# Moving two parts of a modulation product from the end of a recurrent loop to the stage ahead of the attention

## The chip, the cores and the metric

The kernel runs on one core of one Trainium2 chip. The metric is the device time of one execution in microseconds. A core has TensorE (PE), VectorE (DVE), ScalarE (ACT), GpSimd (POOL) and SyncE (SP); each takes its instructions in the order of its own queue. SP here issues nearly all plain transfers, GpSimd the gathers by index; 16 DMA engines carry them.

## The reference

A block of two layers over 512 latent tokens and a prefix of 256 context tokens, width 1024, all in float32. Each layer has six modulation vectors for the latents and six for the context, products of a condition vector with a weight of 1024 x 6144:

```python
for layer in range(DEPTH):                     # 2 layers
    m_l = split((silu(c) @ mod_w[layer] + mod_b[layer]), 6)
    m_c = split( silu(c_ctx) @ mod_w[layer] + mod_b[layer], 6)
    a_l = modulate(rmsnorm(h_lat, norm1_g[layer]), m_l[0], m_l[1])
    a_c = modulate(rmsnorm(h_ctx, norm1_g[layer]), m_c[0], m_c[1])
    # layer 0: RWKV-7 heads and S5 groups; layer 1: latent attention
    o_c, o_l = mixer(a_c, a_l)
    h_lat = h_lat + m_l[2] * o_l
    f_l = modulate(rmsnorm(h_lat, norm2_g[layer]), m_l[3], m_l[4])
    h_lat = h_lat + m_l[5] * moe_ffn(f_l)      # layer 0: context likewise
return rmsnorm(h_lat, final_g)
```

The six vectors of a layer come in three parts of two (2048 columns each): part 0 holds vectors 0 and 1, part 1 holds 2 and 3, part 2 holds 4 and 5.

## The kernel before

The kernel is written in a tile framework. The program gives the order of work; a planner then orders each engine's queue by priority (program order, unless a block raises or lowers it) and by its own estimate of when operands are ready, and puts in the waits. A block under a run-time condition closes the queues: what stands behind it isn't moved ahead of it.

The stages in order of time: `front` (layer 0's modulation, norms, input projection), `rwkv` (six steps of two half steps, with the S5 work and the preparation of later steps in between), `concat`, `ffn(0, ...)` (output projection, router, 20 expert blocks, then `overflow`, a loop under the run-time condition `tc.If(n > 0)`), the stage that prepares the attention, `attention`, `ffn(1, ...)` and the last norm.

`mod_part(l, q, ...)` computes part q of layer l. It clears a bias tile `mb` (GpSimd, one buffer), loads the bias into it, and for 8 slices of the contraction and 2 halves loads a weight tile `mw` of 128 x 4 x 256 (512 KB, pieces of 1 KB) through SP and multiplies it (line 164): four matmuls with a stationary operand of 128 x 32, one for each quarter of TensorE's columns, into one PSUM bank `psmod`. Then `mb` is added, the norm's weight multiplied in, and the rows stored to DRAM (`mods`). In the loop, layer 1's three parts are placed by

```python
MODN = {3: (0,), 4: (1,), 5: (2,)}
```

behind steps 3, 4 and 5, with three buffers for `mw`. Part 0 is read when the attention is prepared, parts 1 and 2 from the output projection of layer 1 on.

A step of the loop needs the inverse of small triangular matrices, made one step ahead in `rwkv_stage_b`: `X` by VectorE row after row (lines 596 and 598), stored by SP (line 601), read back as diagonal blocks `D` (line 604, 16 transfers), then a chain between TensorE and ScalarE: `Ta` (613), `W` (617), `G` (624), `Tb` (634 and 639), `G` (645). `rwkv_steps` uses it: `VU` (699), then the state `Z` (704 and 706), which the next half step begins by decaying (677).

The stage that prepares the attention begins behind `overflow`. It splits the weights (`mla_split`, lines 1600 to 1604), spreads the gate rows (`row_psum`, 1438), and for six token tiles t (two of context, four latent): `fetch` gathers two expert rows per token (GpSimd, line 1415, tiles `cy`, two buffers each), `combine` adds them to `h` (1528 to 1530), SP stores `h` for latents (2014), then the norm (`rstd_of`), its transpose (`norm_tile`, `ntt`), the down projection (`mla_down`) and the value products (`mla_values`). PSUM has eight banks: `tp`, `mm`, `ca` and `cb` with two buffers each.

Of the kernel before, what the change touches and what calls it, by code (L numbers as in the profile page):

```python
# [16 lines left out]
F32 = mybir.dt.float32  # L17
# [27 lines left out]
MS14 = (4, 0, 5, 1, 6, 2, 7, 3, 12, 8, 9, 10, 11, 13)  # L45
MODT = "lo"
S5LATE = -800
MODN = {3: (0,), 4: (1,), 5: (2,)}


def dap(ap, offset, dims):
# [36 lines left out]
class Block:  # L88
# [35 lines left out]
    def cond(self, tp):  # L124
        nc, i = self.nc, self.i
        cr = tp.tile([16, 128], F32, name="cr")
        nc.sync.dma_start(cr[0:8, :], i["c"].rearrange("b (k p) -> (b k) p", p=128))
        nc.sync.dma_start(cr[8:16, :], i["c_ctx"].rearrange("(k p) -> k p", p=128))
        cs = tp.tile([16, 128], F32, name="csil")
        nc.scalar.activation(cs, cr, AF.Tanh, scale=0.5)  # L130
        nc.vector.tensor_scalar(cs, cs, 0.5, 0.5, op0=OP.mult, op1=OP.add)
        nc.vector.tensor_tensor(cs, cs, cr, OP.mult)
        pt = self.psum("tp", "pt_c", 2)
        nc.tensor.transpose(pt[:, :16], cs, self.ident[:16, :16])
        self.cst = self.c0.tile([128, 8, 32], F32, name="cst")
        nc.gpsimd.memset(self.cst, 0.0)
        nc.vector.tensor_copy(self.cst[:, :, 0:2], pt[:, :16].rearrange("p (v k) -> p k v", v=2))

    def mod_part(self, l, q, wpool, spool, tag="mod"):

        nc, i = self.nc, self.i
        if l not in self.mods:
# [13 lines left out]
            nc.vector.tensor_scalar(mb[r0:r0 + 64, :], mb[r0:r0 + 64, :], 1.0, None, op0=OP.add)  # L156
        ps = self.psum(tag, f"psmod{l}{q}", 1)
        for k in range(8):
            for h in range(2):
                wt = wpool.tile([128, 4, 256], F32, name=f"mw{l}{q}{k}{h}", tag="mw")  # L160
                w = i["mod_w"][l, k * 128:(k + 1) * 128, q * 2048:q * 2048 + 2048].rearrange("p (j c) -> p j c", j=4)
                last = nc.sync.dma_start(wt, w[:, :, 256 * h:256 * h + 256])
                for j in range(4):
                    nc.tensor.matmul(ps[32 * j:32 * j + 32, 256 * h:256 * h + 256], self.cst[:, k, :], wt[:, j],  # L164
                                     start=(k == 0 and h == 0), stop=(k == 7), skip_group_check=True)
        mo = mb
        nc.vector.tensor_tensor(mo, ps, mb, OP.add)
# [1263 lines left out]
        nc.vector.tensor_tensor(hh, hh, ps[:, 256:], OP.mult)  # L1431
        return hh

    def row_psum(self, rows, name):

        out = [self.psum("cb", f"{name}{hf}", 2) for hf in range(2)]
        for j in range(8):
            self.nc.tensor.matmul(out[j // 4][:, j % 4 * 128:j % 4 * 128 + 128], self.ident[0:8, j:j + 1].to_broadcast([8, 128]),
                                  rows, start=True, stop=True, skip_group_check=True)
        return out  # L1440
# [174 lines left out]
    def mla_values(self, t):  # L1615

        nc = self.nc
        ts = slice(t * 128, t * 128 + 128)
        for hh in range(2):
            hs = slice(hh * 8, hh * 8 + 8)  # L1620
            ps = self.psum("ca", f"pv{t}{hh}", 2)
            self.mm3(ps, (self.kvT[0][:, ts], self.kvT[1][:, ts]), [x[:, hs, :].rearrange("p h c -> p (h c)") for x in self.kw],
                     True, True)
            dst, src = self.vv[:, t, hs], ps.rearrange("p (h c) -> p h c", h=8)
# [5 lines left out]
    def mla_down(self, aT, t, sp):  # L1630
# [8 lines left out]
        else:  # L1639
            nc.tensor.matmul(ps[:, 0:416], self.tri[0:1, 1], self.mwb, start=True, stop=False)  # L1640
            for k in range(8):
                self.mm3(ps[:, 0:416], (aT[0][:, k], aT[1][:, k]), (self.mwi[0][:, k], self.mwi[1][:, k]), False, k == 7)
        pt = self.psum("cb", f"pmt{t}", 2)
        if t >= 2:
            r = self.rstd_of(sp, ps[:, 0:256], f"mq{t}", 256)
            qn = sp.tile([128, 256], F32, name=f"qn{t}", tag="qn", bufs=2)
            nc.vector.scalar_tensor_tensor(qn, ps[:, 0:256], r, self.qnb, op0=OP.mult, op1=OP.mult)
            for k in range(2):
                nc.tensor.transpose(pt[:, k * 128:(k + 1) * 128], qn[:, k::2], self.ident)
        r = self.rstd_of(sp, ps[:, 256:384], f"mk{t}", 128)  # L1650
        kn = sp.tile([128, 128], F32, name=f"kn{t}", tag="kn", bufs=2)
        nc.vector.scalar_tensor_tensor(kn, ps[:, 256:384], r, self.kvb, op0=OP.mult, op1=OP.mult)
        nc.tensor.transpose(pt[:, 256:384], kn, self.ident)
        pe = sp.tile([128, 32], F32, name=f"kpe{t}", tag="kpe", bufs=2)
# [305 lines left out]
    def build(self):  # L1960
# [7 lines left out]
        with ExitStack() as es:  # L1968
# [10 lines left out]
            with ExitStack() as ec:  # L1979
# [5 lines left out]
        mes = ExitStack()  # L1985
        self.ffn(0, cat, hts, self.src_rows, i["hy_w_out"], ces,
                 lambda: self.mla_weights(self.pool("mlaw", 1, es=mes, side="right")))
        with ExitStack() as e0:
            kp = self.pool("mlk", 1, es=e0)
            self.rq = kp.tile([128, 2, 16, 96], F32, name="mqu")  # L1990
# [7 lines left out]
            with ExitStack() as e1:  # L1998
# [3 lines left out]
                sp = self.pool("mls", 1, es=e1, side="right")  # L2002
                g2c = [bp.tile([128, D], F32, name=f"g2c{v}") for v in range(2)]
                for v in (1, 0):
                    for hf, ps in enumerate(self.row_psum(self.g2r[:, v], f"g2c{v}")):
                        nc.scalar.activation(g2c[v][:, hf * 512:hf * 512 + 512], ps, AF.Copy)
                self.mla_split(wp)

                def normed(t):
                    h = hts[t]  # L2010
                    self.combine(self.fetch(0, t, xp, 2), h, g2c[int(t < 2)],
                                 (nc.vector, nc.vector if t < 2 else nc.gpsimd))
                    if t >= 2:
                        nc.sync.dma_start(self.hb[(t - 2) * 128:(t - 1) * 128], h)
                    r = self.rstd_of(xp, h, f"n1{t}")
                    return self.norm_tile(h, r, t, self.mc1, xp)

                nxt = normed(0)
# [148 lines left out]
```

## Time and profile before

| what | us |
|---|---|
| median of 3 runs (1953.17 to 1964.0) | 1959.4 |
| the profiled execution | 1948.41 |
| its span, first to last instruction | 1946.6 |
| TensorE busy in it | 1563.9 (80%) |
| VectorE busy in it | 1218.9 (63%) |
| granted TensorE clock, mean | 0.88 |

The profile is one execution. Its page gives the busy share of each engine, also in 40 slices of 48.7 us, and the DMA queues. The trace behind it gives windows (busy time of each engine in a stretch, the granted clock as a share of 2.4 GHz, the share of time in which the 16 DMA engines were busy and GB/s), waits (who stood idle for whom), and instructions in order of time. Times of a row count from the span's start.

### The profile page before, as it was taken

Reading aid. Unit: us, or ns where it says so; the run is one execution under the profiler, and the core shown is the slowest. Engines: PE = TensorE matmul, PEld = TensorE weight load, DVE = VectorE, ACT = ScalarE, POOL = GpSimd, SP = SyncE. Lnnn points to the kernel's source line nnn. Section 1 sums busy time; section 2 is a strip of 40 time slices with the busy share of each in tenths; the row PEclk is TensorE's granted clock in tenths of the full one; section 3 lists DMA queues with packets and bytes.
Section 4 is the critical chain, followed back from the end, with each engine's and each line's share of the span. In section 5 each row is a group of like instructions: output and inputs, shape, how many; then the busy total and the mean of one; then the engine's idle time right before and its main releaser. Section 6 shows DMA issues by size and latency. Waiting matters only on the chain. (4 is left out here: it accounts for less than half of the span.)

```text
span 1946.6 us, 32507 instructions
## 1 busy us (share of the span) xinstructions
PE 1563.9 (80%) x12531; PEld 1126.9 (58%) x12531; DVE 1218.9 (63%) x2385; ACT 774.2 (40%) x1434; POOL 701.3 (36%) x700
## 2 busy tenths in 40 slices
PE   5698898558687789649698999949699998789993
PEld 2376767447576655337575666638455556666662
DVE  4799933884866867243754654475678854575544
ACT  4222324334543523132413555433556543335542
POOL 0476802441423414102514233451143353324432
PEclk8688999678898869679899999969799998899997
DMA  8754587723233268743605999852000009349965
GB/s 257 213 174 157 164 275 218 218 60 109 62 88 103 72 223 258 241 170 128 246 33 188 389 354 367 328 175 65 1 1 1 1 0 367 110 168 370 377 230 184
DMA packets 222854, 347.65 MB, mean 179 GB/s; under 512 B 49538, under 2 KB 170296, under 8 KB 207784
## 3 DMA queue, kind: packets, MB, share of 16 engines
q1 hardware_dynamic: 206784, 294.71, 45.4%
q0 software_dynamic: 10080, 44.04, 6.3%
q10 hardware_dynamic: 5832, 6.78, 1.1%
q8 instruction: 100, 1.64, 0.3%
q14 instruction: 58, 0.48, 0.1%
HBM read 279.02 MB, written 66.46 MB: 177 GB/s over the span
## 5 line engine op out<-in xcount | busy, mean ns | idle before, releaser
L164 PE MATMUL psmod<-mw,cst 128*32 128x256 f32 x768 | 83.8, 491 | 43.5 <-DMA mw<-in_mod_w_dram 39.2
L191 PE MATMUL pwi<-aT,wih 128*128 128x256 f32 (+1 forms) x224 | 81.7, 367 | 14.4 <-DVE q L334 7.2
L192 PE MATMUL pwi<-aT,wih 128*128 128x256 f32 (+1 forms) x224 | 81.9, 367 | 0.0
L193 PE MATMUL pwi<-aT,wil 128*128 128x512 f32 (+1 forms) x224 | 81.2, 364 | 0.0
L1784 ACT ACTIVATE P<-st 128x512 f32<-128x512 f32 x96 | 56.9, 596 | 48.7 <-PE st L1782 44.7
L1797 POOL TENSOR_TENSOR sum<-sum,P 128x512 f32<-128x512 f32 x48 | 63.6, 1348 | 27.8 <-ACT P L1784 27.6
L1112 PE MATMUL s5y<-s5tq,s5H 128*96 128x128 f32 x256 | 50.6, 333 | 27.3 <-POOL s5H L1104 15.1
L1415 POOL DMA_INDIRECT xg<-fbuf,rk x36 | 37.8, 1051 | 92.9 <-PE ptx L231 52.3
L572 PE MATMUL pg<-PQ,KB 64*128 64x128 f32 x384 | 54.1, 318 | 18.7 <-ACT ta L501 10.4
L1098 POOL TENSOR_TENSOR s5t<-s5G,s5tq 128x384 f32<-128x384 f32 x16 | 18.0, 1123 | 141.5 <-DVE s5G L1095 121.3
L185 ACT ACTIVATE xT<-ptx 128x512 fp32r<-128x512 f32 x72 | 41.2, 596 | 66.1 <-PE ptx L231 65.0
L164 PEld LDWEIGHTS psmod<-mw,cst 128*32 128x32 f32 x768 | 20.3, 124 | 77.4 <-DMA mw<-in_mod_w_dram 55.7
L186 DVE TENSOR_TENSOR xT<-ptx,xT 128x512 fp32r<-128x512 f32 x72 | 48.2, 688 | 23.1 <-ACT xT L185 22.2
L572 PEld LDWEIGHTS pg<-PQ,KB 64*128 64x128 f32 x384 | 44.1, 211 | 31.2 <-ACT ta L501 10.7
L191 PEld LDWEIGHTS pwi<-aT,wih 128*128 128x128 f32 x224 | 46.2, 208 | 22.3 <-issue 11.4
L1112 PEld LDWEIGHTS s5y<-s5tq,s5H 128*96 128x96 f32 x256 | 37.8, 198 | 35.9 <-POOL s5H L1104 16.8
L1795 POOL TENSOR_TENSOR sum<-P,P 128x512 f32<-128x512 f32 x16 | 20.5, 1300 | 105.3 <-ACT P L1784 105.2
L231 PEld LDWEIGHTS ptx<-ident,xg 128*128 128x128 f32 x288 | 40.6, 192 | 26.6 <-issue 21.0
L1788 PE MATMUL po<-P,vv 128*64 128x512 f32 x192 | 54.3, 617 | 1.1 <-ACT P L1784 1.1
L685 PE MATMUL pU<-Z,PQ 128*64 128x128 f32 x192 | 30.3, 331 | 27.9 <-ACT Z L677 27.7
L231 PE MATMUL ptx<-ident,xg 128*128 128x128 f32 x288 | 42.9, 285 | 10.9 <-issue 7.0
L192 PEld LDWEIGHTS pwi<-aT,wih 128*128 128x128 f32 x224 | 46.1, 206 | 7.8 <-issue 3.1
(1569 smaller groups left out, 5161.0 us busy)
## 6 DMA issues: line engine op xcount, KB each, us to landing
mw<-in_mod_w_dram SPq DMA_DIRECT2D x96, 512.0 KB
yb<-yo SPq DMA_DIRECT2D x36, 512.0 KB
s5tq<-s5t SPq DMA_DIRECT2D x16, 960.0 KB
yb<-zrow SPq DMA_DIRECT2D x16, 512.0 KB
wi<-in_hy_w_in_dram SPq DMA_DIRECT2D x14, 512.0 KB
rk<-qbuf SPq DMA_DIRECT2D x12, 512.0 KB
fbuf<-f SPq DMA_DIRECT2D x10, 512.0 KB
s5t<-s5CP SPq DMA_DIRECT2D x4, 1152.0 KB
```

What stands on the lines that cost most here:

```text
L164: nc.tensor.matmul(ps[32 * j:32 * j + 32, 256 * h:256 * h + 256], self.cst[:, k, :], wt[:, j], start=(k == 0 and h == 0), stop=(k == 7), s ...
L185: nc.scalar.activation(hi, src, AF.Copy)
L186: nc.vector.tensor_tensor(lo, src, hi.bitcast(F32), OP.subtract)
L191: nc.tensor.matmul(out, lh, rh, start=start, stop=False, **kw)
L192: nc.tensor.matmul(out, lh, rl, start=False, stop=False, **kw)
L193: nc.tensor.matmul(out, ll, rh, start=False, stop=stop, **kw)
L231: nc.tensor.transpose(pt[:, k * 128:(k + 1) * 128], a[:, h * 4 + k::8], self.ident)
L572: nc.tensor.matmul(pg[hp][:, m], KB[rs, m, ps2], PQ[rs, m, ps2], start=True, stop=True, skip_group_check=True)
L1112: nc.tensor.matmul(out, H[:, g, d, k, h0:h0 + 96], CP[:, k, d, i0:i0 + 8, :].rearrange("p a b -> p (a b)"), start=False, stop=(d == 1 and ...
L1784: ex = nc.scalar.activation(P, st, AF.Exp, scale=SCALE)
L1788: mm = nc.tensor.matmul(po[64 * x:64 * x + 64], vv[:, kt, h0 + x, :], P, start=(kt == 0), stop=(kt == 5), skip_group_check=True)
L1797: nc.gpsimd.tensor_tensor(sums[x], sums[x], P, OP.add)
```

## The change

Only part 0 stays in the loop. Parts 1 and 2 are computed behind `ffn(0, ...)`, after the weights are split and ahead of the first token tile, with weight tiles of 128 x 4 x 128 (256 KB, pieces of 512 bytes), four a slice, and four buffers. The padded condition vector `cst` lives in a pool that closes before the experts, so its two columns are kept in `cst2` and spread again. A PSUM pool of its own serves the stage: the part's accumulator takes one bank (`md`), `cb` has three buffers and takes the value products in as well, and `ca` is gone. For room in SBUF the squares of three norms are written over tiles that are there already: a gathered tile, `qn` and `kn`.

```diff
-MODN = {3: (0,), 4: (1,), 5: (2,)}
+MODN = {3: (0,)}
...
-        nc.vector.tensor_copy(self.cst[:, :, 0:2], pt[:, :16].rearrange("p (v k) -> p k v", v=2))
-
-    def mod_part(self, l, q, wpool, spool, tag="mod"):
+        self.cs2 = self.cp.tile([128, 8, 2], F32, name="cst2")
+        nc.vector.tensor_copy(self.cs2, pt[:, :16].rearrange("p (v k) -> p k v", v=2))
+        nc.vector.tensor_copy(self.cst[:, :, 0:2], self.cs2)
+
+    def mod_part(self, l, q, wpool, spool, tag="mod", parts=2, bufs=None):
...
-            for h in range(2):
-                wt = wpool.tile([128, 4, 256], F32, name=f"mw{l}{q}{k}{h}", tag="mw")
+            for h in range(parts):
+                n = 512 // parts
+                wt = wpool.tile([128, 4, n], F32, name=f"mw{l}{q}{k}{h}", tag="mw", bufs=bufs)
...
-            ps = self.psum("ca", f"pv{t}{hh}", 2)
+            ps = self.psum("cb", f"pv{t}{hh}", 3)
...
-        pt = self.psum("cb", f"pmt{t}", 2)
+        pt = self.psum("cb", f"pmt{t}", 3)
...
+        mp = self.pool("mwp2", 1, es=mes, side="right")
+        self.cst = mp.tile([128, 8, 32], F32, name="cst1")
+        nc.gpsimd.memset(self.cst, 0.0)
+        nc.vector.tensor_copy(self.cst[:, :, 0:2], self.cs2)
+        self.ppes.close()
+        self.psum_pool(None, "ppm")
...
                 self.mla_split(wp)
+                for q in (1, 2):
+                    self.mod_part(1, q, mp, mp, "md", 4, 4)
...
-                    r = self.rstd_of(xp, h, f"n1{t}")
+                    r = self.rstd_of(xp, h, f"n1{t}", sq=ys[1])
```

## Rows read from the trace of the kernel before

**Rows 1.** The page: DMA engines' busy tenths in 40 slices of the span.

```profile
DMA  8754587723233268743605999852000009349965
```

**Rows 2.** Windows of the loop's end: length, busy us and instructions of each engine.

```profile
757.00:781.00 24.00, 19.32 (x183) 9.30 (x182) 23.52 (x75) 6.40 (x16) 10.56 (x17) 0.91 0.76 242
781.00:802.00 21.00, 14.56 (x203) 8.82 (x203) 7.28 (x15) 2.50 (x3) 5.14 (x5) 0.58 0.63 189
802.00:844.00 42.00, 28.65 (x677) 17.11 (x676) 7.13 (x15) 7.72 (x16) 0.00 (x0) 0.73 0.74 237
844.00:878.00 34.00, 11.38 (x176) 9.06 (x176) 19.09 (x39) 15.79 (x31) 0.81 (x6) 0.72 0.44 157
```

**Rows 3.** Windows, instructions on the modulation's accumulator alone: PE, PEld, DVE busy.

```profile
757.00:802.00 45.00, 15.49 (x129) 3.50 (x128) 0.68 (x1) 0.76 0.70 217
802.00:844.00 42.00, 12.17 (x120) 3.17 (x120) 0.69 (x1) 0.73 0.74 237
sum 87.00, PE 27.67 PEld 6.67 DVE 1.37; mean PE 13.83 PEld 3.33 DVE 0.68
```

**Rows 4.** Waits from 802 to 844: us in total, times, the longest.

```profile
ACT Tb L634 <- PE pt L632: 14.7, 1, 14.7
...
PE psmod L164 <- DMA mw<-in_mod_w_dram: 11.6, 7, 6.1
```

**Rows 5.** Timeline of SP's queue, 690 to 880: start, duration, instruction.

```profile
785.98 4.62 SPq L162 DMA_DIRECT2D mw<-in_mod_w_dram  x2
790.69 7.85 SPq L604 DMA_DIRECT2D D<-xo  x16
```

**Rows 6.** Timeline of ScalarE: an earlier step (two rows), then the last.

```profile
476.81 0.59 ACT L613 ACTIVATE Ta<-pd 128x512 f32<-128x512 f32 x1
...
502.84 1.21 ACT L699 ACTIVATE VU<-pU 64x512 f32<-64x512 f32 x2
...
802.08 0.60 ACT L613 ACTIVATE Ta<-pd 128x512 f32<-128x512 f32 x1 [9.55 <-PE pd L612]
...
837.81 1.21 ACT L699 ACTIVATE VU<-pU 64x512 f32<-64x512 f32 x2 [6.94 <-PE pU L697]
...
844.53 2.44 ACT L677 ACTIVATE Z<-Z,dc 128x128 f32<-128x128 f32 x8
```

**Rows 7.** Windows of the stage that prepares the attention, as in rows 2.

```profile
1276.00:1301.00 25.00, 0.31 (x3) 0.12 (x2) 18.38 (x45) 6.71 (x14) 15.15 (x9) 0.55 0.60 194
1301.00:1330.00 29.00, 24.83 (x115) 23.33 (x116) 23.73 (x57) 7.65 (x22) 17.69 (x12) 0.80 0.58 192
1330.00:1372.00 42.00, 38.39 (x177) 32.96 (x175) 22.09 (x94) 13.52 (x45) 0.20 (x1) 0.96 0.00 1
1269.00:1372.00 103.00, 70.53 (x322) 59.26 (x320) 70.65 (x228) 34.42 (x92) 35.47 (x23) 0.82 0.34 110
```

**Rows 8.** Timeline of PE at the head of that stage.

```profile
1268.59 5.75 PE L1603 MATMUL pmwb<-mwr,mcol 128*1 128x416 f32 x16 [0.30 <-PEq L1504]
...
1301.15 1.06 PE L301 MATMUL ntt<-ntd,h 128*128 128x128 f32 x3 [24.84 <-issue]
```

**Rows 9.** DMA, 328 to 342 (512-byte writes), and SP's issues, 14 to 45.

```profile
DMA packets 7921, 4.00 MB, mean 286 GB/s; under 512 B 112, under 2 KB 7921, under 8 KB 7921
...
14.43 30.50 SPq L162 DMA_DIRECT2D mw<-in_mod_w_dram  x13
```

**Rows 10.** The gathered expert rows, 1255 to 1310: durations min/median/max in ns.

```profile
L1530 POOL TENSOR_TENSOR h<-h,cy x2: 2375/2504/2633, 1297.0 to 1302.9; 128x1024 f32<-128x1024 f32 x2
...
DMA to landing us min/median/max: 4.2/5.4/6.6
```

**Rows 11.** Waits from 757 to 845, as in rows 4.

```profile
PE psmod L164 <- DMA mw<-in_mod_w_dram: 18.6, 13, 6.1
...
POOL mb L146 <- DMA mods<-mb: 10.3, 1, 10.3
```

More of the change, by code (lines that the diff above doesn't have):

```diff
@@ L158, in mod_part @@
         for k in range(8):
-            for h in range(2):
-                wt = wpool.tile([128, 4, 256], F32, name=f"mw{l}{q}{k}{h}", tag="mw")
+            for h in range(parts):
+                n = 512 // parts
+                wt = wpool.tile([128, 4, n], F32, name=f"mw{l}{q}{k}{h}", tag="mw", bufs=bufs)
                 w = i["mod_w"][l, k * 128:(k + 1) * 128, q * 2048:q * 2048 + 2048].rearrange("p (j c) -> p j c", j=4)
-                last = nc.sync.dma_start(wt, w[:, :, 256 * h:256 * h + 256])
+                last = nc.sync.dma_start(wt, w[:, :, n * h:n * h + n])
                 for j in range(4):
-                    nc.tensor.matmul(ps[32 * j:32 * j + 32, 256 * h:256 * h + 256], self.cst[:, k, :], wt[:, j],
+                    nc.tensor.matmul(ps[32 * j:32 * j + 32, n * h:n * h + n], self.cst[:, k, :], wt[:, j],
                                      start=(k == 0 and h == 0), stop=(k == 7), skip_group_check=True)
@@ L1432, in expert_mm, with row_psum @@
         return hh
-    def row_psum(self, rows, name):
-        out = [self.psum("cb", f"{name}{hf}", 2) for hf in range(2)]
+    def row_psum(self, rows, name, tag="cb", bufs=2):
+        out = [self.psum(tag, f"{name}{hf}", bufs) for hf in range(2)]
         for j in range(8):
@@ L1642, in mla_down @@
                 self.mm3(ps[:, 0:416], (aT[0][:, k], aT[1][:, k]), (self.mwi[0][:, k], self.mwi[1][:, k]), False, k == 7)
-        pt = self.psum("cb", f"pmt{t}", 2)
+        pt = self.psum("cb", f"pmt{t}", 3)
         if t >= 2:
-            r = self.rstd_of(sp, ps[:, 0:256], f"mq{t}", 256)
             qn = sp.tile([128, 256], F32, name=f"qn{t}", tag="qn", bufs=2)
+            r = self.rstd_of(sp, ps[:, 0:256], f"mq{t}", 256, sq=qn)
             nc.vector.scalar_tensor_tensor(qn, ps[:, 0:256], r, self.qnb, op0=OP.mult, op1=OP.mult)
@@ L1649, in mla_down @@
                 nc.tensor.transpose(pt[:, k * 128:(k + 1) * 128], qn[:, k::2], self.ident)
-        r = self.rstd_of(sp, ps[:, 256:384], f"mk{t}", 128)
         kn = sp.tile([128, 128], F32, name=f"kn{t}", tag="kn", bufs=2)
+        r = self.rstd_of(sp, ps[:, 256:384], f"mk{t}", 128, sq=kn)
         nc.vector.scalar_tensor_tensor(kn, ps[:, 256:384], r, self.kvb, op0=OP.mult, op1=OP.mult)
@@ L2004, in build @@
                 for v in (1, 0):
-                    for hf, ps in enumerate(self.row_psum(self.g2r[:, v], f"g2c{v}")):
+                    for hf, ps in enumerate(self.row_psum(self.g2r[:, v], f"g2c{v}", "cb", 3)):
                         nc.scalar.activation(g2c[v][:, hf * 512:hf * 512 + 512], ps, AF.Copy)
                 self.mla_split(wp)
+                for q in (1, 2):
+                    self.mod_part(1, q, mp, mp, "md", 4, 4)
                 def normed(t):
                     h = hts[t]
-                    self.combine(self.fetch(0, t, xp, 2), h, g2c[int(t < 2)],
+                    ys = self.fetch(0, t, xp, 2)
+                    self.combine(ys, h, g2c[int(t < 2)],
                                  (nc.vector, nc.vector if t < 2 else nc.gpsimd))
```

## Prediction

> **What bounds the kernel now.** The view to begin with is the page's row of DMA busy tenths [rows 1]: counted from 0, slices 14 to 17 (681 to 876 us, the end of the RWKV loop) stand at 6, 8, 7 and 4, slices 28 to 32 (1363 to 1606 us, the attention) at 0. The bytes that the change moves, 32 tiles of 512 KB or 16.8 MB, are loaded now in the first stretch, and the change puts them just ahead of the second.
>
> Next, the loop's end by windows [rows 2]. From 757 to 781 VectorE is busy 23.5 of 24 us (the triangular inverse for the last step, with the rest of the step before): that stretch is VectorE's. From 781 to 844 VectorE is nearly free (14.4 of 63 us) and ScalarE too, while TensorE is busy 43 of 63. So a chain sets the time there, and TensorE's order in it. The same windows for the modulation matmuls alone [rows 3] give 27.7 us of TensorE from 757 to 844, 12.2 of them behind 802; and the waits from 802 to 844 show TensorE standing 11.6 us more before such a matmul for its tile to land [rows 4]. TensorE takes its instructions in order, so the inverse's small matmuls stand behind both: ScalarE waits 14.7 us for one of them [rows 4].
>
> **What is removed.** The chain of the last step: X is written out, read back as the diagonal blocks (16 loads of D), then Ta, W, G, Tb, Tb, G, VU and Z. Two parts of it pay for the modulation.
> First, SP: it stands 4.6 us at two weight tiles before it can issue the D loads [rows 5]. The stall goes: 790.7 - 786.0 = 4.7 us.
> Second, from Ta (802.1) to the next decay of Z (844.5), 42.4 us [rows 6]. Modulation is in it with 12.2 us of matmuls and 11.6 us of waits, 23.8 together: the most that can come back. The least comes from an earlier step, where the way from Ta to VU took 26.0 us with other work in between, against 35.7 here: 9.7 us. Some of the 23.8 lies beside ScalarE's and VectorE's pieces of the chain; TensorE has little else here, so I take a value near the upper end, 19 us.
> Sum: 4.7 + 19 = about 24 us earlier, bounds 14 and 28.5. Behind it the stretch 844 to 878 keeps its length: its chain is Z, the outputs, their norm and the concatenation, without a modulation tile. Everything behind shifts, the experts too. The 15.5 us of modulation matmuls between 757 and 802 [rows 3] I price at nothing: up to 781 they lie beside VectorE at 98% [rows 2], and to 798 beside the D loads [rows 5]. If that cover were gone, each would cost what it takes.
>
> **What is added.** The same 16.8 MB as 64 tiles of 256 KB, on SP, behind the branch that closes the experts, and their matmuls on TensorE in the stretch 1269 to 1372 that prepares the attention. It is not idle [rows 7]: TensorE is busy 70.5 of 103 us there, and the DMA engines 0.34 of the time, 35 us. TensorE's gaps are one of 25 us (1276 to 1301, the wait for the first expert rows; [rows 7, 8]), then 4.2 and 3.6 us.
> DMA first. The nearest row for 512-byte pieces is a run of writes at 286 GB/s [rows 9]: 16.8 MB take 59 us, and with the 35 there already 94 of 103. The nearest row for this very load is the first part of layer 0: 13 tiles of 512 KB in 30.5 us, 2.35 us each, three in flight [rows 9]; by bytes that is 75 us for 64 halves, and 110 with the other traffic. With the first tiles out at about 1269, the stream ends between 1363 and 1379. I take 1368.
> TensorE next, which ends later. The matmuls have half the columns and twice the number, so their time stays 27.7 us [rows 3]. 70.5 + 27.7 = 98.2. In the gap of 25 us the gathers hold 0.60 of the DMA engines [rows 7]; the rest brings 0.40 x 25 x 286 = 2.9 MB, a sixth of the stream, 4.7 us of matmuls: 20.3 us stay empty. Of the later 7.8 us half is filled: 4 stay. 1269 + 98.2 + 24.3 = 1391.5, which is 19.5 later than 1372. On top come waits for tiles that arrive later than the order of TensorE's queue assumed: in the loop's end they were 18.6 us for the same bytes [rows 11], here most of them fall into the gap that is counted already; I take 5. Sum: 24.5 us later. It agrees with the stream: two of the four latent tiles left at 1368, at 42 / 4 = 10.5 us each [rows 7], end at 1389.
> Bounds: from below, all of the 27.7 us falls into the 32.5 us of gaps and the stream ends at 1363 with one tile to come: 2 us. From above, a stream of 113 us (first rival) with three tiles to come: 1269 + 2 for the first landing + 113 + 31.5 = 1415.5, 43 us.
>
> **The smaller edits.** The copy of the condition vector and the memset of its padded form are one small instruction each, beside the branch's first matmul of 5.8 us [rows 8]; without that cover they cost under 1 us. The PSUM banks: value products and the transposed latents now share three buffers instead of two and two. From below nothing; from above as much again as TensorE waits in 1330 to 1372 today, 3.6 us [rows 7]. The modulation's stream covers it; I take nothing. The squares are now written over a gathered tile, so its buffer comes free one addition (2.5 us on GpSimd) and one square later, for a gather that takes 5.4 us to land [rows 10]: at most four times 2.5 us, under the same cover; nothing again, and it is inside the upper bound.
> Nothing behind the attention moves: the parts are read only in the output projection after it, and the DMA engines are idle during the attention [rows 1].
>
> **Sum.** 24 us earlier, 24.5 later: no change. The profiled execution, 1948.4 us, would stay at 1949; it lies 11 us below the median of the runs, 1959.4, and carried to the median the forecast is 1960. Under 0.5%, some 10 us, a measurement of this kernel can hardly be told from no change.
>
> **The rivals.**
> 1. Slower: the stream goes by the count of tiles, not by bytes. Three in flight at 2.35 us each mean that one buffer's round (issue, landing, matmul, release) took 7.05 us [rows 9]. If the round does not shrink with the tile, four in flight give 1.76 us each, 113 us for 64, and the stage ends 43 us later: 43 - 24 = 19, 1978 us. It decides from a round of about 6.5 us on. For it: buffers that come free in the order of a busy TensorE, and the gathers on the same engines. Against it: 512-byte pieces at 286 GB/s. The Trainium skill speaks for it too (DMA: Bandwidth & Descriptors, Rules for kernel authors): for full bandwidth it asks for at least 1 MiB per DMA, and these shrink from a half to a quarter of that. The formula on the same page (Anatomy of one DMA), 2.0 us plus bytes over 436 GB/s, gives as an estimate 64 x 2.6 / 4 = 42 us against 32 x 3.2 / 3 = 34, so 8 us more and 1968; by the 512-byte row alone halving costs nothing. No row here shows a 256-KB tile of this kind.
> 2. Slower: GpSimd. The second of the two parts clears the same bias tile that the first still has to store; that memset waited 10.3 us in the loop's end [rows 11], where GpSimd had nothing to do. Now the expert rows' gathers and the additions on GpSimd stand behind it. If it lies ahead of the last of them, the price is that wait: 10 us, 1970.
> 3. Faster: the matmuls fit the gaps. If the gathers yield more of the DMA engines, most of the 27.7 us goes into the 25 us, and the stage ends some 5 us later: 5 - 24 = -19, 1940. For it: the 25 us are wholly empty, and DMA has 68 us to spare. Against it: the spare DMA time lies mostly behind 1330, TensorE's mostly before 1301.
>
> **Chances.** Forecast 0.40, by itself 1950 to 1969; first rival 0.20, second 0.13, third 0.27. Faster 0.28, no change 0.39, slower 0.33. The range holds the faster rival (1940) and the first one (1978) with some room on each side for the gain's own bounds, 14 and 28.5: 1936 to 1985. Outside lie only the cases where gain and loss are both at opposite ends (1933 and 1988).
>
> **What would show it.** In the profile after: D loads issued right behind X without a tile's stall, and Ta to the decay of Z some 23 us instead of 42; 844 to 878 unchanged in length. Then, from the end of the branch to the attention's first projections, 127 us instead of 103, with modulation matmuls of about 28 us in TensorE's busy time and some 20 us of the first gap still empty. The stream's length decides between forecast and first rival, a wait of the bias tile's memset before a gather shows the second, a full first gap the third. The prediction is wrong if the chain of the last step is held by something that hides now behind the tiles (then the gain falls toward 14), or if TensorE waits for tiles far more than 5 us outside the first gap.

## The result, and the profile after

| | before | after |
|---|---|---|
| median of 10 runs each, us | 1954.3 (1948.7 to 1964.0) | 1972.3 (1964.2 to 1977.4) |
| ratio, with its 95% interval | | 1.008 (1.0057 to 1.0102) |
| the profiled execution, us | 1948.41 | 1972.32 |

The change makes the kernel slower, by 0.8%. A second measurement of both (the last experiment) gave 1.0061 (1.0039 to 1.0084). Both intervals exclude no change; their lower ends are at 0.4 and 0.6%. Lines of the changed kernel stand 3 to 12 higher than in the kernel before (modulation matmul 167, its load 165, Ta 616, VU 702, Z 680).

**How to compare the two traces.** The order of instructions is the same in both (but for small instructions at the very start, and neighbours in TensorE's queue that change places) up to 741.8 us of the kernel before, where its loads of part 1 begin. Yet the second VU of step 3 stands at 652.1 in the one and at 660.6 in the other, and the second VU of step 4 at 748.8 and 760.0, 11.2 us apart. Over thirteen profiles of this study the latter lies anywhere from 747.7 to 765.7 (run 2, whose profiled execution was its longest, has 773.7). So the ends of two profiles say little here, and lengths between fixed instructions say more. Three stretches carry the change: *loop's end*, from the second VU of step 4 to the second VU of step 5; *experts*, from there to TensorE's first instruction behind the branch; *stage*, from there to the first projection of the attention.

| us | before | after |
|---|---|---|
| loop's end | 101.6 | 83.0 |
| experts | 418.2 | 424.0 |
| stage | 109.1 | 132.4 |
| first projection to the first gather of layer 1 | 349.6 | 351.7 |

The prediction ended the stage at the copies of the attention's first weights; by that mark it is 103.4 and 131.9 us, so 28.5 more instead of 23.3. In before these copies ran 5.7 us ahead of the first projection, which is the row that counts:

```profile
1377.66 0.76 PE L191 MATMUL pqp<-qT,qwp 128*128 128x512 f32 x1 [0.83 <-ACT ngm L1687]
```

**The loop's end after**, by windows, cut at the steps of the chain; columns as in [rows 2].

```profile
757.00:781.00 24.00, 18.55 (x224) 13.26 (x223) 20.71 (x65) 12.36 (x25) 5.99 (x9) 0.89 0.27 85
781.00:794.00 13.00, 5.38 (x25) 4.67 (x24) 12.62 (x29) 0.00 (x0) 8.03 (x11) 0.63 0.24 81
794.00:806.50 12.50, 4.98 (x138) 4.03 (x137) 5.27 (x12) 2.50 (x3) 1.50 (x2) 0.50 0.17 22
806.50:837.00 30.50, 19.72 (x561) 16.43 (x560) 6.07 (x13) 7.24 (x15) 0.00 (x0) 0.61 0.23 76
837.00:870.00 33.00, 12.00 (x177) 9.68 (x176) 18.48 (x38) 15.56 (x32) 0.20 (x2) 0.71 0.45 162
```

From 781 to 837 TensorE is busy 30 of 56 us, and the DMA engines move 65 GB/s on average, under a third of the 221 that [rows 2] give from 781 to 844. Timelines of the same stretch: SP's queue and ScalarE, as in [rows 5, 6], then TensorE. The bracket is the engine's idle time before the instruction and what ended it.

```profile
794.34 1.11 SPq L604 DMA_DIRECT2D xo<-X  x2
796.29 7.43 SPq L607 DMA_DIRECT2D D<-xo  x16
...
821.17 8.87 SPq L1957 DMA_DIRECT2D cy<-rwbuf  x4
```

```profile
806.55 0.60 ACT L616 ACTIVATE Ta<-pd 128x512 f32<-128x512 f32 x1 [7.95 <-PE pd L615]
...
828.69 1.29 ACT L648 ACTIVATE G<-pt 32x256 f32<-32x256 f32 x4 [7.76 <-PE pt L645]
832.03 1.21 ACT L702 ACTIVATE VU<-pU 64x512 f32<-64x512 f32 x2 [2.05 <-PE pU L700]
836.80 2.44 ACT L680 ACTIVATE Z<-Z,dc 128x128 f32<-128x128 f32 x8 [3.56 <-DVE Z L709]
```

```profile
817.78 1.92 PE L640 MATMUL pt<-Tb,G 32*32 32x32 f32 x64 [1.27 <-ACT Tb L637]
825.71 1.08 PE L1960 MATMUL ptcat<-ident,cy 128*128 128x128 f32 x4 [6.01 <-DMA cy<-rwbuf]
826.73 1.92 PE L645 MATMUL pt<-G,Tb 32*32 32x32 f32 x64
```

The D loads go out right behind X: the stall is gone. From Ta to the decay of Z it is now 30.3 us, against 42.4 in [rows 6]. What is left is not all chain: TensorE stands 6.0 us before `ptcat`, a transpose of the concatenation that waits for its transfer `cy<-rwbuf` (issued at 821.17), and the chain's matmul of line 645 is queued behind it, so ScalarE's G waits 7.8 us.

**The first expert gather.** Timelines of the kernel after where the experts begin: SP, then GpSimd, then ScalarE.

```profile
1026.43 0.98 SPq L165 DMA_DIRECT2D mw<-in_mod_w_dram  x2
...
1028.00 1.06 SPq L165 DMA_DIRECT2D mw<-in_mod_w_dram  x2
```

```profile
1033.38 1.16 POOL L1418 DMA_INDIRECT xg<-fbuf,rk  x1 [0.30 <-POOL h L1276]
```

```profile
1042.79 0.60 ACT L188 ACTIVATE xT<-ptx 128x512 fp32r<-128x512 f32 x1 [15.60 <-PE ptx L234]
```

Four of the 64 weight tiles, a megabyte, go out 240 us ahead of TensorE's first instruction behind the branch, just before the first gather of token rows. The first transposed token tile comes 9.4 us behind that gather's issue. In the trace of before the same way takes 5.7 us (1042.38 to 1048.10).

**The stage after**, by windows, to be held against [rows 7], and its last row for the modulation's accumulator alone:

```profile
1267.00:1277.00 10.00, 10.00 (x46) 4.33 (x47) 7.57 (x34) 6.75 (x12) 5.46 (x4) 0.83 0.67 187
1277.00:1300.00 23.00, 14.25 (x143) 8.83 (x141) 14.93 (x46) 5.59 (x11) 8.98 (x6) 0.63 0.90 283
...
1310.00:1330.00 20.00, 16.88 (x105) 13.96 (x105) 9.36 (x31) 5.67 (x14) 6.63 (x6) 0.88 1.00 335
1330.00:1357.00 27.00, 27.00 (x181) 22.17 (x184) 17.23 (x67) 8.71 (x30) 2.92 (x2) 0.96 0.34 101
1357.00:1372.00 15.00, 15.00 (x147) 11.11 (x140) 5.88 (x22) 3.91 (x13) 0.00 (x0) 1.00 0.49 142
1372.00:1391.00 19.00, 14.99 (x146) 6.60 (x145) 5.49 (x23) 4.16 (x13) 0.39 (x3) 0.64 0.82 236
1391.00:1399.00 8.00, 1.74 (x24) 0.56 (x24) 2.89 (x4) 0.26 (x2) 3.52 (x5) 0.66 0.25 71
1267.00:1399.00 132.00, 108.14 (x856) 74.70 (x856) 71.36 (x236) 36.85 (x98) 36.55 (x31) 0.82 0.67 206
```

```profile
1267.00:1399.00 132.00, 30.16 (x512) 12.31 (x512) 1.38 (x2) 0.82 0.67 206
```

The timeline of SP's queue in it, and from the waits of that queue the longest (us, times, longest):

```profile
1277.53 22.04 SPq L165 DMA_DIRECT2D mw<-in_mod_w_dram  x15
1300.22 0.34 SPq L2026 DMA_DIRECT2D hbuf<-h  x1
1304.62 4.09 SPq L165 DMA_DIRECT2D mw<-in_mod_w_dram  x5
...
1315.99 7.97 SPq L165 DMA_DIRECT2D mw<-in_mod_w_dram  x4
...
1328.08 18.14 SPq L165 DMA_DIRECT2D mw<-in_mod_w_dram  x4
...
1349.78 2.84 SPq L165 DMA_DIRECT2D mw<-in_mod_w_dram  x4
1352.67 1.12 SPq L174 DMA_DIRECT2D mods<-mb  x2
1354.36 0.37 SPq L165 DMA_DIRECT2D mw<-in_mod_w_dram  x1
1356.72 1.11 SPq L150 DMA_DIRECT2D mb<-in_mod_b_dram  x2
1357.93 33.49 SPq L165 DMA_DIRECT2D mw<-in_mod_w_dram  x27
1396.57 1.06 SPq L174 DMA_DIRECT2D mods<-mb  x2
```

```profile
SPq L165 <- PE psmod L167: 68.7, 44, 11.9
```

Three phases are to be seen. To 1300 the tiles go out at 1.5 us each, in TensorE's first gap. From 1300 to 1357 TensorE is full with the token tiles (27.0 of 27 us from 1330 on), and only 18 tiles go out, 3.2 us each: a buffer is still waiting for its matmuls, which stand in TensorE's order behind token work (68.7 us of SP's time between 1225 and 1400). From 1358 the last 27 tiles go out, one every 1.27 us; up to 1372 TensorE is still full (15.0 of 15 us), and from there it waits for them, with the last token tile's matmuls queued between them. The end, by the timelines of ScalarE and TensorE:

```profile
1389.59 0.60 ACT L1631 ACTIVATE vv<-pv 128x512 f32<-128x512 f32 x1 [3.26 <-PE pv L196]
...
1398.89 0.81 ACT L188 ACTIVATE qwp<-mqu 128x256 fp32r<-128x256 f32 x3 [7.74 <-DMA mods<-mb]
```

```profile
1393.64 1.41 PE L167 MATMUL psmod<-mw,cst 128*32 128x128 f32 x16 [0.44 <-DMA mw<-in_mod_w_dram]
1399.36 0.80 PE L194 MATMUL pqp<-qT,qwp 128*128 128x512 f32 x1 [4.30 <-ACT qwp L188]
```

The last value products are copied out at 1389.6; the attention's first weights wait 7.7 us, and the trace puts that down to the store of part 2, `mods<-mb`. The attention doesn't read part 2; its first weights are tiles of a pool that opens when the stream's pool, with its weight and bias tiles, has closed. Run 7 tests the store.

### The profile page after: what moved, and what is told of

Its sections match the earlier page's. It is cut to its first block, busy times and chain, and to the rows that moved or that the text cites. A ratio compares the mean times of both kernels' runs of the same rounds, so it can differ in the third digit from the quotient of the medians.

```text
span 1970.5 us, 33089 instructions
## 1 busy us (share of the span) xinstructions
PE 1594.2 (81%) x12787; PEld 1152.1 (58%) x12787; DVE 1216.3 (62%) x2387; ACT 774.7 (39%) x1434; POOL 701.6 (36%) x701
## 5 line engine op out<-in xcount | busy, mean ns | idle before, releaser
L167 PE MATMUL psmod<-mw,cst 128*32 128x256 f32 (+1 forms) x1024 | 84.9, 410 | 41.7 <-DMA mw<-in_mod_w_dram 36.8
L194 PE MATMUL pwi<-aT,wih 128*128 128x256 f32 (+1 forms) x224 | 82.0, 369 | 12.2 <-DVE s5w L994 7.4
L1115 PE MATMUL s5y<-s5tq,s5H 128*96 128x128 f32 x256 | 55.5, 358 | 36.0 <-POOL s5H L1105 18.4
L167 PEld LDWEIGHTS psmod<-mw,cst 128*32 128x32 f32 x1024 | 25.4, 121 | 80.5 <-DMA mw<-in_mod_w_dram 57.8
L1115 PEld LDWEIGHTS s5y<-s5tq,s5H 128*96 128x96 f32 x256 | 41.8, 216 | 43.2 <-POOL s5H L1105 19.5
L195 PEld LDWEIGHTS pwi<-aT,wih 128*128 128x128 f32 x224 | 46.7, 209 | 7.5 <-issue 3.1
L1761 DVE TENSOR_REDUCE mxp<-sc 128x1 f32<-128x512 f32 x64 | 43.0, 684 | 12.7 <-PE sc L1760 12.1
```

The lines of the kernel that those rows point to most:

```text
L167: nc.tensor.matmul(ps[32 * j:32 * j + 32, n * h:n * h + n], self.cst[:, k, :], wt[:, j], start=(k == 0 and h == 0), stop=(k == 7), skip_gr ...
L194: nc.tensor.matmul(out, lh, rh, start=start, stop=False, **kw)
L195: nc.tensor.matmul(out, lh, rl, start=False, stop=False, **kw)
L1115: nc.tensor.matmul(out, H[:, g, d, k, h0:h0 + 96], CP[:, k, d, i0:i0 + 8, :].rearrange("p a b -> p (a b)"), start=False, stop=(d == 1 and ...
L1761: V.tensor_reduce(part[:, 2 * j + x:2 * j + x + 1], sc, AX.X, OP.max)
```

## Experiments

Each was timed against the kernel before on the same chip. The stretches are from each one's own profile, of one execution; the sum of their differences to before, with the stretch behind the stage, agrees with the ratio to a quarter of a per cent, 5 us (run 4: -10 us, 0.995; run 6: +17 us, 1.009; run 10, the furthest off: +16 us, 1.008 against 1.006). A few us in one stretch of one profile are to be read with that in mind.

| run | ratio (95%) | loop's end | experts | stage |
|---|---|---|---|---|
| before | 1 | 101.6 | 418.2 | 109.1 |
| after | 1.008 (1.0057 to 1.0102) | 83.0 | 424.0 | 132.4 |
| 1 edits only | 0.998 (0.995 to 1.001) | 98.8 | 419.9 | 104.6 |
| 2 parts left out | see there | 83.6 | 419.1 | 108.0 |
| 3 loads, no matmuls | 1.003 (1.000 to 1.006) | 82.7 | 422.6 | 127.0 |
| 4 matmuls, no loads | 0.9945 (0.991 to 0.9979) | 82.5 | 423.9 | 111.5 |
| 5 part 2 only | 0.9968 (0.994 to 0.9996) | 88.8 | 420.3 | 113.6 |
| 6 big tiles | 1.0105 (1.0052 to 1.0158) | 85.3 | 420.7 | 140.7 |
| 7 store released | 1.0012 (0.9986 to 1.0039) | 83.3 | 419.1 | 126.3 |
| 8 one step sooner | 0.9992 (0.9968 to 1.0015) | 104.1 | 420.0 | 107.8 |
| 9 half bytes | 1.000 (0.997 to 1.003) | 84.2 | 421.5 | 125.2 |
| 10 first tiles gated | 1.006 (1.0037 to 1.0083) | 84.3 | 419.6 | 139.1 |
| 11 part 2, gated, released | 0.9964 (0.9938 to 0.9991) | 89.9 | 421.0 | 113.5 |
| 12 after again | 1.0061 (1.0039 to 1.0084) | 83.0 | 422.4 | 130.4 |

**1. The edits without the move.**

```diff
-MODN = {3: (0,)}
+MODN = {3: (0,), 4: (1,), 5: (2,)}
...
-                for q in (1, 2):
-                    self.mod_part(1, q, mp, mp, "md", 4, 4)
```

> All edits of the change but the move: the three parts stay in the loop, the stage ahead of the attention has the new PSUM pool, the squares written over other tiles and the second copy of the condition vector. My prediction priced these at nothing: 1954 us like before, within 3. Rival: the squares over a gathered tile let each gather begin one addition and one square later, which nothing hides now that no modulation stream is there: up to four times 2.5 us, 1964, and the expert rows of the last tokens land up to 10 us later in the trace.

Measured: 0.998. The small edits cost nothing, as priced; the rival (gathers 10 us late) falls. In its profile the stage is even 4.5 us shorter than before; held against it, the move costs the stage 26 to 28 us. Run 2's stage, with the same edits and no stream either, is 108.0; against that it is 22 to 24.

**2. Parts 1 and 2 left out.**

```diff
-                for q in (1, 2):
-                    self.mod_part(1, q, mp, mp, "md", 4, 4)
+                nc.sync.dma_start(dap(self.mods[1], 2048, [[6 * D, 2], [1, 4096]]),
+                                  dap(self.mods[0], 2048, [[6 * D, 2], [1, 4096]]))
```

> The kernel after, but parts 1 and 2 of layer 1 are not computed at all: the rows of layer 0 are copied in their place (one small transfer), so the output differs; the removal from the loop and all other edits stay. My prediction: the gain at the loop's end by itself, 24 us, 1930 (bounds 14 and 28.5: 1940 and 1926). What the trace of the kernel after shows at the loop's end is less, a lead that changes by 18.7 us from 749 to 850: 1935. Rival: the removal gains less than that at the end of the kernel, because the experts behind it give part back (in the trace of the kernel after the lead shrank by 5.9 us there): 1941.

Measured: 1969.9 us, ratio 1.0065, which can't be read as it is. With the copied rows the tokens of layer 1 choose other experts, and the loop under the branch, which runs not once in layer 1 of the kernel before, runs once here (GpSimd gathers its weights at 1925.23): from the first gather of layer 1 to the end it is 253.7 us instead of 219.3. Without these 34.4 us the median would be about 1935.5, 22 below the 1957.7 of before, an estimate, since the 34.4 are from its profiled execution, the longest of its twelve. So only the stretches are read: the loop's end is 83.6 us, a gain of 18.0, the lower of the two numbers expected, and the experts give nothing back (419.1).

**3 and 4. Loads without matmuls, matmuls without loads.**

```diff
 run 3
-                for j in range(4):
-                    nc.tensor.matmul(ps[32 * j:32 * j + 32, n * h:n * h + n], self.cst[:, k, :], wt[:, j],
+                for j in range(4 if parts == 2 or k == 0 else 1):
+                    c = n if parts == 2 or k == 0 else 8
+                    nc.tensor.matmul(ps[32 * j:32 * j + 32, n * h:n * h + c], self.cst[:, k, :], wt[:, j, :c],
 run 4
-                last = nc.sync.dma_start(wt, w[:, :, n * h:n * h + n])
+                if first:
+                    last = nc.sync.dma_start(wt, w[:, :, n * h:n * h + n])
```

> The kernel after with all 64 weight tiles of parts 1 and 2 loaded, but 56 of them multiplied by one matmul of 8 columns instead of four of 128 (so the two parts hold one eighth of their sum): the transfers without the matmul time. If TensorE's time sets the stage, as my accounting had it (98 us of matmuls and 24 of gaps), the loads alone end before the last token tile and cost little: 1930 to 1945. If the stream of tiles sets it (the first rival: a round per buffer, 113 us from 1269), the stage stays as long as in the kernel after: 1965 to 1972.

> The kernel after with all 512 matmuls of parts 1 and 2, but only the first four weight tiles of each part loaded and used again for the other slices (so the two parts hold one slice's product): the matmul time without the transfers. If TensorE's time alone sets the stage, it costs 27.7 us less what fits the first gap of 25 us, some 5 us: 1940. If the cost lies in tiles that come late, as in my accounting (20 us of the first gap stay empty for want of tiles) and in the first rival, then it is small here too, 1935 to 1945. Only if matmuls can't use the gap, because of their place in TensorE's order, does it stay near 1960 to 1972.

Measured: 1962.7 and 1942.4 us, the first between the two times that were named for it, the second as expected. (With other sums in the parts layer 1 could choose other experts; from its first gather to the end both take 219.2 us, as before.) With the loads alone the stage keeps 127.0 us, with the matmuls alone 111.5, against 104.6 (run 1) or 108.0 (run 2) with neither. So 22 of the 28 us, or 19 of the 24, come with the loads, and the accounting by TensorE's time is refuted: TensorE is free of the modulation and still waits. Run 3's waits, and the end of its stage on ScalarE, say for what:

```profile
PE psmod L168 <- DMA mw<-in_mod_w_dram: 25.9, 26, 3.0
```

```profile
1382.17 0.60 ACT L1632 ACTIVATE vv<-pv 128x512 f32<-128x512 f32 x1 [3.93 <-PE pv L197]
...
1397.47 0.81 ACT L189 ACTIVATE qwp<-mqu 128x256 fp32r<-128x256 f32 x3 [13.74 <-DMA mods<-mb]
```

TensorE stands 25.9 us before the short matmuls that release the tiles. For a part of them the token work stands behind: the last value products are copied out 111.2 us into the stage, against 103.4 in run 1 and 106.7 in run 2. The larger part of the loss comes after that: from there to the first projection it is 15.8 us, against 1.2 in both. In that time the stream's last tiles land and part 2 is stored, and the attention's first weights wait 13.7 us for the store, to take the place of the stream's tiles in SBUF. In the kernel after it is 9.8 us.

**5. Part 2 alone moved.**

```diff
-MODN = {3: (0,)}
+MODN = {3: (0,), 4: (1,)}
...
-                for q in (1, 2):
+                for q in (2,):
```

> Only part 2 is moved (32 tiles of 256 KB, four in flight), part 1 stays behind step 4 of the loop. Theory now: the gain of the move sits in the last step's chain, where part 2's matmuls and their waits lie (24 us from Ta to the decay of Z), while part 1's lie beside VectorE and the transfers of D: most of the 18 us that the loop's end gave for both parts stays, 14 to 18. The cost was the stream being held by four buffers whose release stands in TensorE's order behind the token tiles; 32 tiles end long before the last token tile, so the stage costs some 8 us instead of 23 to 28, and the early tiles cost 3 to 4 us at the first expert gather as before: ratio 0.995 to 1.000. Rival: gain and cost are both proportional to the tiles moved (9 us gained, 12 to 14 lost, 4 at the gather): ratio 1.004.

Measured: 0.9968, and so faster than before, by 0.04 to 0.6%. The gain at the loop's end is 10 to 13 us (88.8 against 101.6 and 98.8), between theory and rival; the stage costs 4.5 to 9. Its profile parts the two terms of the gain: from Ta to the decay of Z it takes 30.6 us, as in the kernel after (30.3), but with part 1 still in the loop the D loads come 6.3 us behind X (2.0 in the kernel after, 7.8 in before). So the time behind Ta was part 2's alone, and the stall of SP stays as long as part 1 is there.

**6 and 9. The size of the tile, and its bytes.**

```diff
 run 6
-                    self.mod_part(1, q, mp, mp, "md", 4, 4)
+                    self.mod_part(1, q, mp, mp, "md", 2, 2)
 run 9
-                last = nc.sync.dma_start(wt, w[:, :, n * h:n * h + n])
+                m = 4 if parts == 2 else 2
+                last = nc.sync.dma_start(wt[:, :m], w[:, :m, n * h:n * h + n])
...
-                                     self.cst[:, k, :], wt[:, j],
+                                     self.cst[:, k, :], wt[:, j % m],
```

> The kernel after with 32 tiles of 512 KB, two in flight, instead of 64 of 256 KB, four in flight: the same bytes in flight, half the transfers and pieces twice as long. First rival of the prediction (the stream goes by count of tiles, and small transfers are dear): the stage gets shorter by 8 us and more, ratio 1.004 or less. Theory now (a tile's round is set by where its matmuls stand in TensorE's order, not by its transfer): no gain, with only two buffers rather a loss; ratio 1.006 to 1.012, as the kernel after, 1.008.

> The kernel after with each of the 64 tiles loaded to half (two of its four column blocks, 128 KB), and the four matmuls of a tile reading those two twice (so the parts hold other sums): the same count of transfers, the same pieces, the same matmuls, half the bytes. If bytes set the stream, the stage from the branch's end to the first projection falls by 10 us and more, from 132 to 120 or less, and the ratio to 1.003 or less. If the count of tiles or their buffers' round in TensorE's order sets it, the stage stays at 128 to 134 and the ratio at 1.006 to 1.01.

Measured: big tiles 1.0105, stage 140.7; half the bytes 1.000, stage 125.2. The two together tell what a tile costs. SP's queue for part 2 in run 9 (128 KB, four in flight) and run 6 (512 KB, two in flight):

```profile
1342.00 32.19 SPq L166 DMA_DIRECT2D mw<-in_mod_w_dram  x28
```

```profile
1355.36 36.78 SPq L165 DMA_DIRECT2D mw<-in_mod_w_dram  x14
```

From issue to issue that is 1.18 and 2.80 us, and 1.27 in the kernel after; times the tiles in flight, a buffer's round (from one load's issue to the next into the same buffer) is 4.7 us at 128 KB, 5.1 at 256 KB and 5.6 at 512 KB on average. These averages hide a difference: up to 1358 TensorE was full with token work in run 9 (16.0 of 16 us), and its rounds there took 5.2 to 6.7 us whatever the load. Where TensorE was no longer full (issues from 1360 on in run 9, from 1372 in the other two) the mean round was 3.7, 4.7 and 5.5 us, the shortest 2.6, 3.8 and 4.7. So the round grows with the size, but only by half for four times the bytes, and big tiles with two buffers lose. Run 9's stage is 5 to 7 us shorter and lies between the two that were named, the 120 us of a stream bound by bytes and the 128 of one bound by count or round. Its ratio of 1.000 is the one named for bytes; by the stretches it is +4 us, 0.2%, inside the interval, and 4 to 8 us less than the kernel after, of which 5 to 7 in the stage.

**7. The store kept off the attention.**

```diff
+        mps = ExitStack()
+        ms = self.pool("msp2", 1, es=mps)
         mp = self.pool("mwp2", 1, es=mes, side="right")
...
-                    self.mod_part(1, q, mp, mp, "md", 4, 4)
+                    self.mod_part(1, q, mp, ms, "md", 4, 4)
```

> The kernel after with the bias tile and the norm's weight (from which the rows are stored) in a pool that stays open through the attention, so that the attention's first weights no longer wait for the store of part 2, but only for its last matmul. In the trace of the kernel after that wait ended last: 7.7 us of ScalarE before the first attention weights, of which 4.5 us lie behind the last modulation matmul. Theory: the attention starts 4 to 5 us earlier, ratio 1.006 against 1.008. Rival: the first projections are held by the last six weight tiles in TensorE's order anyway, nothing changes.

Measured: 1.0012, more than expected. The stage is 4 to 6 us shorter, as the theory has it. But the attention's first weights still wait, now for the last modulation matmul, which reads the last weight tile:

```profile
1378.79 0.81 ACT L188 ACTIVATE qwp<-mqu 128x256 fp32r<-128x256 f32 x3 [10.97 <-PE psmod L167]
```

The last value products are copied out 113.0 us into this stage, the first projection comes at 126.3. Neither needs part 2; to keep the weight tiles (and the PSUM bank) apart as well, so that the attention can begin before the stream ends, was not tried. The rest of the gain is in the experts, 419.1 instead of 422.4 and 424.0. With the new pool the bias and norm rows go out behind the branch instead of ahead of the first gather, but that gather still waits 7.7 us; whether they are the cause stays open.

**8. One step sooner, nothing moved out of the loop.**

```diff
-MODN = {3: (0,), 4: (1,), 5: (2,)}
+MODN = {3: (0, 1), 4: (2,)}
```

> The kernel before with the parts one step sooner in the loop: parts 0 and 1 behind step 3, part 2 behind step 4, nothing behind step 5, and nothing moved to the stage ahead of the attention. Theory: the last step's chain gets free as in the kernel after (18 us), and what the sooner parts cost depends on the stretch from 690 to 757, where TensorE is full and at half its clock for a part of it: 27.7 us of matmuls less what lies beside VectorE from 757 to 802. I expect 8 to 14 us lost there: ratio 0.995 to 0.998. Rival: TensorE's order in step 4 pays as much as step 5 did, ratio 1.000 or more; other rival: all of it hides, 0.990.

Measured: 0.9992, no change, and the loop's end stays at 104.1. The edit hardly moved the work: the first load of part 1 goes out 7.3 us ahead of the second VU of step 4 (7.0 in before), and the first matmul of part 2 runs 46.0 us behind it (46.7). Placed a step sooner in the program, the matmuls still fill the last step, so neither the theory nor the rivals, which say what a sooner place would pay, were put to the test.

**10. The first tiles held until the branch is over.**

```diff
+                if dep is not None and k == 0:
+                    nc.vector.tensor_copy(wt[:, 0, 0:1], dep)
...
-                    self.mod_part(1, q, mp, mp, "md", 4, 4)
+                    self.mod_part(1, q, mp, mp, "md", 4, 4, g2c[1][:, 0:1] if q == 1 else None)
```

> The kernel after with one addition: into each of the first four tiles VectorE copies one column of a row that is only there behind the branch, so these four loads can't go out in the middle of the experts (where they did, at 1026 us, ahead of the first expert gather). Theory: in all six kernels that sent tiles there, the first transposed expert tile came 7.7 to 9.4 us behind the first gather, against 5.7 to 6.0 in the four that didn't; with the gate it is back at 6, worth 2 to 3.6 us. Against it the four tiles then land behind the branch, at most 4 us of stream: ratio 1.006 to 1.008, and the mechanism is read from the trace. Rival: the early loads have nothing to do with it (it is the bias and norm loads or the memsets), the wait stays at 8 to 9 us.

Measured: 1.006, with 1.0061 for the kernel after in the same comparison. The mechanism is confirmed: the first transposed tile comes 5.74 us behind the gather, though the bias and norm rows still go out early. In all, six of six kernels that sent whole tiles there waited 7.7 to 9.4 us (8.2 in the second profile of the kernel after), those that sent none 5.7 to 6.0, and run 9, with half the bytes, 6.4. But held back, the tiles make the stage 7 to 9 us longer (139.1), and the ratio is the same, so nothing is won.

**11. The version that the others point to**: run 5 with the gate of run 10 and the pool of run 7.

```diff
-                for q in (1, 2):
-                    self.mod_part(1, q, mp, mp, "md", 4, 4)
+                for q in (2,):
+                    self.mod_part(1, q, mp, ms, "md", 4, 4, g2c[1][:, 0:1])
```

> The version that the other runs point to: only part 2 moved, its first four tiles held until the branch is over, its bias tile in a pool that stays open through the attention. From the run with only part 2 moved (0.9968): the early tiles no longer delay the first gather (2.5 us), the store no longer matters. Theory: 0.995, between 0.992 and 0.998. Rival: tiles that start later cost the stage what the gather gains, 0.997 or more.

Measured: 0.9964, within the expected bounds and no better than run 5, which doesn't tell theory from rival. The gather is back at 5.7 us, the stage unchanged. Both runs beat both kernels, the one before by little (0.04 to 0.6%, 0.1 to 0.6%); run 5 is the simpler one.

**12. The changed kernel again**, with no edit.

> The changed kernel once more, for a second profile and more runs. Theory: ratio 1.008 within its interval, 1.006 to 1.010; 749 to 850 shortened to 83 us, the branch's end to the first projection 132 us. The 11 us by which the first profile was late already at 749, with the same order of instructions, come from the clock granted in that execution and need not come again; if they do come again with the parts gone from step 4, the removal itself costs clock there.

Measured: 1.0061, loop's end 83.0, stage 130.4. The point at the second VU of step 4 lay at 761.8 this time, again late; but of this second delay 90.4 us fall between the second VU of step 3 and that point, against 99.4 in the first profile and 96.7 in before, so it doesn't arise in the same place.

## Why the prediction was right in its range and wrong in its steps

The forecast was no change, 1960; the truth is slower by 0.6 to 0.8%, inside the range and on the side of the slower rivals. By stretches the two profiles of the kernel after give -18.6 at the loop's end, +5.8 and +4.2 in the experts, +23.3 and +21.3 in the stage, +2.1 and +1.0 behind it: 12.6 and 8.0 us, 0.65 and 0.4%. The runs measured 0.8 and 0.6%, and the few us between aren't placed.

**The gain, 24 us: failed by 5.** (By 8 against run 1, whose loop's end is 98.8.) The first term held: the D loads go out 5.6 us earlier against VU, where 4.7 was reckoned. The second, 19 of the 23.8 us between Ta and the decay of Z, did not: it gave 12.2. I had read 9.7 as the least, from an earlier step, and set it aside because "TensorE has little else here". That step was the better row: from Ta to VU it took 26.0 us there, and 25.5 in the kernel after. What I took for little is the concatenation, whose transposes stand in TensorE's order ahead of the chain's matmul and wait 6.0 us for their own load; the same wait is there in the profiles of the other kernels without part 1 and 2 in the loop (4.3 to 5.8 us), and in none of before, run 1 and run 8. It is the case that the prediction named as its failure, something that hid behind the tiles. Taking it away was not tried. Behind the chain the length stayed, as forecast: from the decay of Z to the next transposes of the concatenation it is 15.0 us in before and 15.2 in after.

**The early tiles: missing.** I reckoned with first tiles at 1269, taking the branch for a wall that nothing behind it passes, as the section on the kernel before has it. For loads without an operand behind the branch it isn't one: four tiles went out at 1026 and delayed the first gather by 2 to 3.7 us. Run 10 shows the cause of that; the experts took 4 to 6 us longer, and the rest isn't placed.

**The stage, 24.5 us: the number came near, by luck; the working did not hold.** Measured, 23.3 and 21.3 to the first projection, and 28.5 and 26.5 to the copies of the first weights, where the prediction had put its mark. But it was summed as TensorE's busy time plus gaps, and run 3 shows that the stage is nearly as long without those matmuls. Of the pieces, the stream's end was set at 1368 and came at 1391; 20 us of the first gap were to stay empty, and from 1277 to 1300 it was 8.8; 5 us of waits for tiles were 16. The errors happened to cancel. What holds the stage is a circle that my sum left out: a buffer is released by matmuls that stand behind token work in TensorE's order, and that delays the next load; when the tokens are nearly done, 27 tiles are left, and TensorE waits for them one round at a time. And the attention waits for the stream's end, which the sum had only as token tiles still to come: the tokens were done 122.6 and 120.2 us into the stage, the first projection came 9.8 and 10.2 us later (1.2 in before), though it reads neither part: by the waits, and by run 7, its weights take the place of the stream's tiles. A kernel that keeps the two apart was not tried.

**The rivals.** The first was right in part of its mechanism and wrong in its size. A tile's round grows far less than its bytes, but it is 5.1 us and not 7.05, so the stream alone would take 64 x 1.27 = 81 us, not 113; the rest was TensorE's order, which the rival named as speaking for it. The Trainium skill's formula (DMA: Bandwidth & Descriptors, Anatomy of one DMA; it is stated for GpSimd's path) has a fixed 2.0 us for a transfer and the bytes on top, as an estimate 0.3 us more from 128 to 256 KB and 0.6 more from there to 512 KB; the mean rounds with TensorE not full grew by 1.0 and 0.8 us, with the matmul in them. The Trainium skill's rule of at least 1 MiB per DMA (same page, Rules for kernel authors) was not tested: on the way to 512 KB no gain was to be seen, but the buffers in flight were halved for it. The second rival came in part: the memset of the bias tile waited 9.4 us for the store, but behind all gathers; it kept only SP, 3.6 us from the last tile before it to the first behind it. The third, matmuls in the first gap, was half right: 8.2 of the 30.2 us went there.

**The smaller edits** were rightly priced at nothing (run 1).

**Left open.** Whether the change reaches the time ahead of the second VU of step 4 at all. That point lies at 747.7 to 755.8 in the three profiles with all parts in the loop, and at 749.2 to 765.7 in the ten others (run 2 left out); the groups overlap, and up to there TensorE multiplies almost only part 0 in all of them.

## What to carry to other kernels

Work moved into a gap is not priced by its busy time alone: ask which instruction releases its buffers and what stands ahead of that instruction in its engine's order, since a stream with few buffers gets one tile per (round of a buffer) / (buffers), and the round here grew by half for four times the bytes. Ask too who takes the buffers' place afterwards: here the attention, which reads nothing of the stream, waited for its end. Where a stall is taken off a chain, take what comes back from another occurrence of the same chain without the stall, not from the stall's own length: something else may be queued in the same place, as it was here. And a moved load can start much earlier than the block in which it is written; look for what it meets there.

## What was not expected of the hardware

A buffer's round, from one load's issue to the issue of the next into the same buffer, took on average 3.7 us at 128 KB, 4.7 at 256 KB and 5.5 at 512 KB where TensorE was no longer full (runs 9, after and 6): four times the bytes made it half as long again.

And executions with nearly the same order of instructions drift apart. In before and after the second VU of step 3 stands 8.5 us apart, and TensorE's granted clock was 0.97 between 625 and 650 us in the one and 0.52 in the other. Ten microseconds of it, before and then after, show the two levels, 2.4 and 1.2 GHz:

```profile
630.00:640.00 10.00, 8.38 (x96) 7.14 (x97) 3.46 (x8) 4.15 (x11) 2.47 (x7) 1.00 0.48 168
```

```profile
630.00:640.00 10.00, 10.00 (x99) 8.68 (x99) 1.02 (x2) 1.87 (x5) 4.09 (x9) 0.50 0.41 135
```

In the ten microseconds ahead of it TensorE was busy 9.0 us in the one and 8.1 in the other. Runs 3 and 4, with the same order up to there, stood 16.5 us apart at the second VU of step 4 (765.7 and 749.2).
